# Seven products instead of eight for the first token block of a feed-forward down projection, with the up weights' sums made earlier

## The chip, the core and the metric

The kernel runs on one core of a Trainium2 chip. The metric is the device time of one execution in microseconds; lower is better. The engines that appear below are TensorE (PE; its weight loads are listed as PEld), VectorE (DVE), ScalarE (ACT), GpSimd (POOL) and SyncE (SP), which issues every DMA of this kernel.

## The reference

One layer of a hybrid encoder trunk runs over 2048 prompt positions and 32 sample positions (2080 columns here), with a width of 1024 and a hidden width of 4096, in float32:

```
h = RMSNorm(x) * (1 + scale1) + shift1        # shift, scale, gate from silu(c) @ ada_w + ada_b
p = h @ w_in                                  # mixer A: u, v; mixer B: q, k, v, z, a, b
A = u * (W_s v + b_s)                         # blocks of 128 positions
B = gated delta rule over chunks, gated RMSNorm
x = x + gate1 * (concat(A, B) @ w_out)
h = RMSNorm(x) * (1 + scale2) + shift2
x = x + gate2 * (relu(h @ w_up)^2 @ w_down)   # 1024 -> 4096 -> 1024
y = RMSNorm(x)
```

The change concerns the last product pair, `w_up` and `w_down`.

## The kernel before

**Precision.** A float32 operand of a large product is split into a high part, rounded to fp32r by a ScalarE copy, and a low part, which VectorE makes by a subtraction (`split`, `operand`). `mm3` multiplies high by high, high by low and low by high: three matmuls for one product.

**Stages.** `startup` makes the conditioning of the first normalization and the first projections. `mixers` goes through two halves of the sequence: at the head of `v_stage(0)` come the rest of the conditioning (`ada(1)`, `ada(2)`, `scale_col`), then the projections slab by slab (weights of 512 KB are loaded into `raws` and split into `wh` and `wl`), the delta rule (`delta_local`, `delta_inv` on POOL, `delta_chain`), and at the end the output projection `out_stage` of both halves. Mixer tiles are places in 25 slots of SBUF that rings hand out.

**Feed-forward.** `feed_forward` takes four token blocks b = 0 to 3 of 520 columns, each as two groups of 260. Matrices are cut into 2x2 quadrants, and a product of 2x2 by 2x2 quadrants takes seven block products instead of eight, by Winograd's form of Strassen's scheme: some sums of quadrants are multiplied instead of the quadrants, and the results are added. An up step `up(b, s)`, 16 of them, always takes seven products. For that it needs three quadrants of `w_u[s]` as they are and four sums of quadrants. In block 0 `up_weights` loads the four quadrants, POOL makes the sums, ScalarE and VectorE split them, and the high and low parts are stored to the DRAM tensors `su_d`; blocks 1 to 3 load these parts and ScalarE copies them into `uw`.

A down stage q of a block (8 of them, two half-stages u each) takes the hidden values of two up steps. `plain(b, q)` says which way it goes. All stages of block 0, and stage 7 of every block, go by `ffn_down8`: eight products, with the hidden quadrants as operands. The others go by `ffn_down`: seven products, for which `hidden` also makes the differences T1 to T4 of hidden tiles on POOL, and `down_sums` loads sums of quadrants of `w_d` from `sd_d`. These sums are made by POOL and stored: for even u in block 0 (inside `down_weights`), for odd u in block 1 (inside `down_sums`). Results are added in `add` from PSUM to `acc` by VectorE (in stage 0 the first ones are ScalarE copies). Banks of PSUM are taken and given back (`take`, `give`), eight in all. Normalized inputs of the next block are made at up step 8 (`h2_values`) and loaded and split after step 15 (`h2_load`).

**Order.** Every operation is first recorded with an engine, an estimated duration, and what it reads and writes (`Program.op`). Then `schedule` plays the engines by these estimates and puts each engine's instructions in the order of that play; this order is fixed, and each engine, SP included, follows it. Among operations that are ready the lower rank goes first:

```
CHAIN, INV, LOCAL, EVAC, GEMM, IDLE = range(6)
key = [(o.prio, due[i] if o.prio >= EVAC else i, i) ...]
```

`due` is the position of the first matmul of rank GEMM that depends on the operation. A DMA is estimated at its bytes divided by 360 bytes per ns, at least 500 ns, with 3.5 us until it lands. In the profile, instructions of these helpers have the helper's line: ScalarE L337, VectorE and POOL `tt` L352, `ts` L366, DMA L390, matmuls L398, transposes L409. Tiles tell stages apart: `g` is the PSUM of projections, `f` that of the feed-forward, C and L and B and M those of the mixers' small products; `s` is a slot, `wh`, `wl` and `wr` are places in the slab buffers and the slab staging tile.

Of the kernel before, what the change touches and what calls it, by code (L numbers as in the profile page):

```python
# [16 lines left out]
P = 128  # L17
# [37 lines left out]
CHAIN, INV, LOCAL, EVAC, GEMM, IDLE = range(6)  # L55

# [62 lines left out]
class View:  # L119
# [55 lines left out]
    def pbc(self, n):  # L175
        return self.step("partition_broadcast", np.broadcast_to(np.uint8(0), (n,) + self.shape), self.reg, n)

# [145 lines left out]
class Kern:  # L323
# [61 lines left out]
    def dma(self, out, in_, n=None):  # L385
# [4 lines left out]
        self.p.op(DMA, max(500, x), lambda: nc.sync.dma_start(out=R(out), in_=R(in_)), [out], [in_], lat=DMA_LATENCY + min(0, x - 500))  # L390
# [144 lines left out]
    def setup(self):  # L535
# [74 lines left out]
        rg("va", [(q, 256 * e) for q in (18, 19, 20) for e in range(4)][:10], (P, 256))  # L610
        rg("raw", hv(18), (P, 516))
# [24 lines left out]
        self.su_d = [[[dt(f"su_d{s}_{i}{e}", [P, 512]) for e in range(2)] for i in range(4)] for s in range(16)]  # L636
# [52 lines left out]
    def consts(self):  # L689
# [3 lines left out]
        with self.p.at(GEMM):  # L693
# [19 lines left out]
            self.fill(self.z0, 0.0)  # L713

# [208 lines left out]
    def v_stage(self, hf):  # L923
# [506 lines left out]
    def up_weights(self, b, s):  # L1430

        quad = lambda q: self.i["w_u"][s, q]
        if b == 0:
            a11, a12, a21, a22 = (self.raw(self.uraw, quad(q)) for q in range(4))
            s1, s2 = (self.turn(self.uraw) for _ in range(2))
            self.tt(s1, a21, a22, ALU.add, POOL)
            self.tt(s2, s1, a11, ALU.subtract, POOL)
        out = []

        def sum_(i, x):  # L1440
            if b == 0:
                hl = self.operand(self.uw, x)
                for e in range(2):
                    self.dma(self.su_d[s][i][e], hl[e].f32())
            else:
                hl = self.turn(self.uw)
                for e in range(2):
                    self.act(hl[e], self.raw(self.uraw, self.su_d[s][i][e]), AF.Copy)
            out.append(hl)

        plain = lambda q, x: out.append(self.operand(self.uw, x if b == 0 else self.raw(self.uraw, quad(q))))
        if b:
            s1 = s2 = s3 = s4 = a11 = a12 = a22 = None
        plain(0, a11)
        sum_(1, s2)
        sum_(0, s1)
        if b == 0:
            s3 = self.turn(self.uraw) if len(self.uraw) > 6 else a11
            self.tt(s3, a11, a21, ALU.subtract, POOL)
        sum_(2, s3)  # L1460
        if b == 0:
            s4 = s2
            self.tt(s4, a12, s2, ALU.subtract, POOL)
        sum_(3, s4)
        plain(1, a12)
        plain(3, a22)
        return out

    def down_weights(self, b, u):

        quad = lambda q: self.i["w_d"][u, q]
        if self.plain(b, u // 2):
            a = [self.raw(self.draw, quad(q)) for q in range(4)]
            out = [self.operand(self.dw, x) for x in a]
            if b == 0 and u % 2 == 0 and u < 14:
                a11, a12, a21, a22 = a
                for i, (o, x, y, op) in enumerate(((a22, a21, a22, ALU.add), (a21, a11, a21, ALU.subtract),
                                                   (a11, a22, a11, ALU.subtract), (a12, a12, a11, ALU.subtract))):
                    self.tt(o, x, y, op, POOL)
# [366 lines left out]
```

## Time and profile before

| | us |
|---|---|
| median of 3 runs | 2394.3 (2388.73 to 2394.79) |
| the profiled execution, time | 2384.64 |
| its span | 2382.9 |
| TensorE busy | 2342.0 (98%) |
| VectorE, ScalarE, POOL busy | 1722.2, 1543.3, 752.3 |
| DMA | 570.37 MB, mean 239 GB/s |

Busy time of TensorE is the time in which at least one matmul was under way. Rows of a group read: line, engine, operation, output and input tiles, shape and count, then busy us and the mean ns of one instruction, then the engine's idle time just before them and what ended it. Rows of a stretch give from:to, its length, busy us and instruction count of TensorE, its weight loads, VectorE, ScalarE and POOL, then the granted clock, the share of time that the 16 DMA engines were busy, and GB/s. Rows of a tile give a count, min/median/max ns and the first and last start in us. Rows of waits give the total us, how many times, and the longest. Rows of DMA issues give the count, the size and the median us from issue to landing.

### The profile page before, as it was taken

The page shows a single profiled execution, that of the slowest core. Times are in us where ns is not written, and L with a number is a line of the kernel's source. Part 1 is how long each engine was busy: PE and PEld are TensorE (multiplying, and loading weights), DVE is VectorE, ACT ScalarE, POOL GpSimd, SP SyncE. Part 2 cuts the span into 40 slices and gives each one's busy share as a digit, 9 for nine tenths or more (in the row PEclk, how much of TensorE's full clock was granted, in tenths as well). Part 3 has the DMA queues.
Part 4 walks back from the last instruction along what each step waited for, and adds up shares of the span by engine and source line. Part 5 has one row for each costly group of instructions (what it writes and reads, how often), then busy time and mean ns, then how long its engine had stood idle before and what let it go on. Part 6 is the DMA issues. An engine that isn't in the chain of part 4 may idle for free.

```text
span 2382.9 us, 53525 instructions
## 1 busy us (share of the span) xinstructions
PE 2342.0 (98%) x18834; PEld 2203.8 (92%) x18834; DVE 1722.2 (72%) x3993; ACT 1543.3 (65%) x3703; POOL 752.3 (32%) x1055
## 2 busy tenths in 40 slices
PE   7999999999999999999999999999999999999998
PEld 4877878999999878999999999999999999999998
DVE  5556666556664656487767778989888888778796
ACT  4555557455565434366554688787898778887774
POOL 2134421312423223354434363323531211611111
PEclk9999999999999999999999999999999999999999
DMA  8688658555457867888766778787889778886773
GB/s 310 213 288 296 215 183 261 146 185 173 152 161 231 248 200 230 270 273 273 267 228 216 255 249 302 245 299 240 289 268 297 262 251 273 251 261 225 241 238 109
DMA packets 387237, 570.37 MB, mean 239 GB/s; under 512 B 71356, under 2 KB 201296, under 8 KB 386968
## 3 DMA queue, kind: packets, MB, share of 16 engines
q1 hardware_dynamic: 386968, 566.96, 73.2%
q8 instruction: 148, 2.42, 0.4%
q14 instruction: 121, 0.99, 0.1%
HBM read 432.44 MB, written 134.35 MB: 238 GB/s over the span
## 4 chain that ended last, share of the span: by engine, by line
PE 79%; DVE 6%; DMA 6%; ACT 4%; issue 3%; POOL 2%; SPq 0%; POOLq 0%; DVEq 0%; ACTq 0%
PE f L398 43%; PE g L398 27%; PE C L398 3%; DVE s L352 3%; ACT s L337 2%; PE B L398 2%; POOL s L352 2%; PE L L398 1%; PE M L398 1%; DVE wl L352 1%; DVE s L357 1%; PE L L409 1%; ACT wh L337 1%; DMA s<-su_d 1%; DVE BL L352 1%
## 5 line engine op out<-in xcount | busy, mean ns | idle before, releaser
L337 ACT ACTIVATE s<-s 128x260 f32<-128x260 f32 (+8 forms) x1379 | 601.5, 463 | 327.9 <-DVE s L357 90.7
L398 PE MATMUL f<-s,s 128*128 128x260 f32 x4068 | 535.5, 283 | 0.4 <-DVE s L352 0.4
L398 PE MATMUL f<-BH,wh 128*128 128x260 f32 x1796 | 510.7, 284 | 5.4 <-DVE s L352 4.3
L352 POOL TENSOR_TENSOR s<-s,s 128x260 f32<-128x260 f32 (+3 forms) x354 | 356.8, 1019 | 488.1 <-ACT s L337 364.6
L398 PEld LDWEIGHTS f<-s,s 128*128 128x128 f32 x4068 | 507.2, 188 | 0.8 <-DVE s L352 0.6
L398 PE MATMUL f<-BH,wl 128*128 128x260 f32 x1796 | 507.7, 283 | 0.2 <-DVE wl L352 0.2
L398 PE MATMUL f<-BL,wh 128*128 128x260 f32 x1796 | 506.4, 282 | 0.1
L352 DVE TENSOR_TENSOR s<-s,s 128x512 fp32r<-128x512 f32 (+5 forms) x721 | 402.6, 572 | 64.6 <-ACT s L337 42.1
L352 DVE TENSOR_TENSOR s<-f,s 128x260 f32<-128x260 f32 x856 | 348.1, 420 | 118.9 <-PE f L398 109.9
L398 PE MATMUL g<-BH,wh 128*128 128x512 f32 (+2 forms) x1112 | 421.7, 379 | 0.6 <-ACT BH L337 0.4
L398 PE MATMUL g<-BH,wl 128*128 128x512 f32 (+2 forms) x1112 | 392.1, 353 | 0.0
L398 PE MATMUL g<-BL,wh 128*128 128x512 f32 (+2 forms) x1112 | 390.9, 352 | 0.9 <-DVE BL L352 0.9
L398 PEld LDWEIGHTS f<-BH,wh 128*128 128x128 f32 x1796 | 337.8, 188 | 7.9 <-DVE s L352 2.7
L398 PEld LDWEIGHTS f<-BH,wl 128*128 128x128 f32 x1796 | 338.3, 188 | 0.9 <-DVE wl L352 0.8
L398 PEld LDWEIGHTS f<-BL,wh 128*128 128x128 f32 x1796 | 338.5, 188 | 0.3 <-DVE BL L352 0.3
L352 POOL TENSOR_TENSOR s<-s 128x260 f32<-128x260 f32 (+11 forms) x315 | 157.8, 501 | 474.5 <-DVE s L352 201.1
L337 ACT ACTIVATE wh<-s 128x512 fp32r<-128x512 f32 (+1 forms) x369 | 229.7, 629 | 54.0 <-PE f L398 16.3
L398 PEld LDWEIGHTS g<-BH,wh 128*128 128x128 f32 x1112 | 210.6, 189 | 29.3 <-issue 9.3
L398 PEld LDWEIGHTS g<-BH,wl 128*128 128x128 f32 x1112 | 209.7, 189 | 19.4 <-issue 0.2
L398 PEld LDWEIGHTS g<-BL,wh 128*128 128x128 f32 x1112 | 210.9, 190 | 16.0 <-DVE BL L352 1.7
L398 PE MATMUL f<-BH,s 128*128 128x260 f32 x1016 | 224.6, 283 | 0.0
L357 DVE SCALAR_TENSOR_TENSOR s<-s,s,s 128x400 f32<-128x400 f32 (+6 forms) x318 | 164.2, 532 | 57.2 <-ACT s L337 36.4
(119 smaller groups left out, 3517.4 us busy)
## 6 DMA issues: line engine op xcount, KB each, us to landing
s<-su_d SPq DMA_DIRECT2D x288, 256.0 KB, 3.7
s<-w_u SPq DMA_DIRECT2D x171, 256.0 KB, 3.8
s<-w_d SPq DMA_DIRECT2D x151, 256.0 KB, 4.5
s<-sd_d SPq DMA_DIRECT2D x106, 256.0 KB, 4.1
wr<-su_d SPq DMA_DIRECT2D x96, 256.0 KB, 3.9
wr<-w_b SPq DMA_DIRECT2D x42, 512.0 KB, 4.3
wr<-w_d SPq DMA_DIRECT2D x70, 256.0 KB, 4.6
s<-x_d SPq DMA_DIRECT2D x128, 130.0 KB, 3.8
```

Of the source, the lines that this page charges most:

```text
L337: self.p.op(ACT, c, lambda: nc.scalar.activation(out=R(out), in_=R(in_), func=func, **{k: R(v) for k, v in kw.items()}), [out, accum], [in ...
L352: self.p.op(eng, c, lambda: e.tensor_tensor(out=R(out), in0=R(a), in1=R(b), op=op), [out], [a, b])
L357: self.p.op(DVE, c, lambda: nc.vector.scalar_tensor_tensor(out=R(out), in0=R(a), scalar=R(s), in1=R(b), op0=op0, op1=op1), [out], [a, s, b])
L398: nc.tensor.matmul(R(out), R(l), R(r), **kw)
L409: self.p.op(PE, 114, lambda: nc.tensor.transpose(R(out), R(in_), R(ident)), [out], [in_, ident])
```

## The change

1. A new `up_sums` makes the four sums of each `w_u[s]` within the mixers. It is recorded after the conditioning and its loads depend on it (`after`). Its loads have rank LOCAL, its other operations rank IDLE. Column slices of 128 are loaded, VectorE makes the sums in place and they are stored as float32 to `su_d[s][0]`; ScalarE rounds a copy, VectorE subtracts it, and the low parts go to `su_d[s][1]`. Two load places (slot 4) and four places for the low parts, in free corners of slots 8, 9, 10 and 14, are used in turn.
2. `up_weights` is the same in all blocks: three quadrants are loaded and split; for four sums two tiles are loaded and copied by ScalarE.
3. `plain` holds only for stage 7, so stages 0 to 6 of block 0 go by `ffn_down` with seven products. `down_sums` makes and stores all sums of `w_d` in block 0, for even and odd u, and block 1 loads them.
4. The differences in `hidden` run on VectorE in block 0 and on POOL in the others.
5. The staging tiles `uraw` and `draw` are one ring of eight from the start; block 0 uses the operand rings `rpa` and `rpb` of the other blocks.
6. A DMA is estimated at 330 bytes per ns in place of 360.

```diff
-        x = b / 360
+        x = b / 330
...
+        rg("sh", [(8, 512), (9, 0), (10, 768), (14, 784)], (P, 2, 128))
+        rg("sx", [(4, 0), (4, 512)], (P, 4, 128))
...
+    def up_sums(self, after):
+        for n in range(64):
+            s, c = n // 4, slice(128 * (n % 4), 128 * (n % 4) + 128)
+            x = self.new("sx")
+            with self.p.at(LOCAL):
+                self.dma(x, self.i["w_u"][s, :, :, c].rearrange("q p c -> p q c"), after=after)
+            a11, a12, a21, a22 = (x[:, q] for q in range(4))
+            self.tt(a22, a21, a22, ALU.add)
+            self.tt(a21, a11, a21, ALU.subtract)
+            self.tt(a11, a22, a11, ALU.subtract)
+            self.tt(a12, a12, a11, ALU.subtract)
+            self.dma(self.su_d[s][0][:, :, c], x)
+            for h in (slice(2, 4), slice(0, 2)):
+                y = self.new("sh")
+                self.cp(y.f32r(), x[:, h], ACT)
+                self.tt(y, x[:, h], y, ALU.subtract)
+                self.dma(self.su_d[s][1][:, h, c], y)
...
             self.scale_col(self.a2, 4, 1)
+            with self.p.at(IDLE):
+                self.up_sums((len(self.p.ops) - 1,))
...
+        for i, q in ((None, 0), (0, None), (3, None), (2, None), (1, None), (None, 1), (None, 3)):
+            if i is None:
+                out.append(self.operand(self.uw, self.raw(self.uraw, self.i["w_u"][s, q])))
+                continue
+            hl = self.turn(self.uw)
+            for e in range(2):
+                self.act(hl[e], self.raw(self.uraw, self.su_d[s][e][:, i]), AF.Copy)
...
-        if b == 1 and u % 2:
+        if b == 0:
             a11, a12, a21, a22 = (get(quad(q)) for q in range(4))
...
-    def plain(self, b, q):
-        return b == 0 or q == 7
+    def plain(self, q):
+        return q == 7
...
-        self.uraw = two(0) + two(1) + two(2)
-        self.draw = [self.raw1[0][:, 512 * e : 512 * e + 512] for e in range(2)] + two(21)
+        self.uraw = self.draw = [self.raw1[0][:, 512 * e : 512 * e + 512] for e in range(2)] + two(21) + two(0) + two(1)
...
+        eng = POOL if b else DVE
         if s % 2 == 0 and g == 0:
             put("B11", t)
-            self.tt(k0, k1, t, ALU.subtract, POOL)
+            self.tt(k0, k1, t, ALU.subtract, eng)
```

More of the change, by code (lines that the diff above doesn't have):

```diff
@@ L383, in transpose32, with dma @@
         self.p.op(DVE, 68 + 1.042 * out.n, lambda: nc.vector.transpose(R(out), R(in_)), [out], [in_])
-    def dma(self, out, in_, n=None):
+    def dma(self, out, in_, n=None, after=()):
         nc = self.nc
@@ L1428, in operand, with up_weights @@
         return hi, lo
[L1430 to L1437, printed above, removed]
-        out = []
[L1440 to L1448, printed above, removed]
-            out.append(hl)
[L1451 to L1466, printed above, removed]
+    def up_weights(self, s):
+        out = []
+        for i, q in ((None, 0), (0, None), (3, None), (2, None), (1, None), (None, 1), (None, 3)):
[5 more added lines that the diff above has]
+                self.act(hl[e], self.raw(self.uraw, self.su_d[s][e][:, i]), AF.Copy)
+            out.append(hl)
         return out
@@ L1471, in down_weights @@
         quad = lambda q: self.i["w_d"][u, q]
[L1472 to L1479, printed above, removed]
-                    self.dma(self.sd_d[u][(0, 2, 1, 3)[i]], o)
-            return out
+        if self.plain(u // 2):
+            return [self.operand(self.dw, self.raw(self.draw, quad(q))) for q in range(4)]
         return self.down_sums(b, u)
```

40 lines of the change are left out of this document (20 added, 20 removed).

## Prediction

> **What bounds the kernel now.** I read the page first: busy time by engine, then the chain that ended last.
>
> ```profile
> PE 2342.0 (98%) x18834; PEld 2203.8 (92%) x18834; DVE 1722.2 (72%) x3993; ACT 1543.3 (65%) x3703; POOL 752.3 (32%) x1055
> PE 79%; DVE 6%; DMA 6%; ACT 4%; issue 3%; POOL 2%; SPq 0%; POOLq 0%; DVEq 0%; ACTq 0%
> PE f L398 43%; PE g L398 27%; PE C L398 3%; DVE s L352 3%; ACT s L337 2%; PE B L398 2%; POOL s L352 2%; PE L L398 1%; PE M L398 1%; DVE wl L352 1%; DVE s L357 1%; PE L L409 1%; ACT wh L337 1%; DMA s<-su_d 1%; DVE BL L352 1%
> ```
>
> TensorE is nearly always busy and carries 79% of the chain; over half of that is the feed-forward products (tile f). So a matmul taken away counts in full as long as the others keep up. Where token blocks begin is seen in the first use of an up weight after a gap (rows of tile f and of tile wh in short windows):
>
> ```profile
> L398 PE MATMUL f<-BH,wh x27: 278/283/389, 1029.4 to 1039.8; 128*128 128x260 f32 x27
> L398 PE MATMUL f<-BH,wh x3: 282/282/285, 1379.2 to 1379.9; 128*128 128x260 f32 x3
> L398 PE MATMUL f<-BH,wh x2: 277/280/282, 1709.4 to 1709.8; 128*128 128x260 f32 x2
> L398 PE MATMUL f<-BH,wh x3: 282/283/285, 2040.2 to 2040.9; 128*128 128x260 f32 x3
> ```
>
> The blocks last 349.8 us (b=0), 330.2 (b=1) and 330.8 (b=2). The next rows are busy time by stage: the mixers after the conditioning, blocks 0, 1 and 2, then shorter stretches.
>
> ```profile
> core 0: us, PE busy (x) PEld busy (x) DVE busy (x) ACT busy (x) POOL busy (x), PEclk, DMA share, GB/s
> 220.00:985.00 765.00, 757.44 (x6234) 680.31 (x6233) 467.01 (x1357) 417.68 (x1157) 231.19 (x514) 1.00 0.65 203
> 1030.00:1376.00 346.00, 342.90 (x2846) 341.20 (x2845) 265.64 (x488) 202.91 (x463) 147.94 (x117) 1.00 0.76 253
> 1376.00:1707.00 331.00, 329.70 (x2739) 328.16 (x2738) 287.50 (x602) 269.60 (x617) 128.34 (x131) 1.00 0.83 272
> 1707.00:2038.00 331.00, 329.31 (x2734) 327.84 (x2733) 278.86 (x604) 269.09 (x628) 90.59 (x106) 1.00 0.83 268
> 1200.00:1300.00 100.00, 100.00 (x837) 100.00 (x836) 70.77 (x140) 51.11 (x114) 36.17 (x27) 1.00 0.66 229
> 2100.00:2300.00 200.00, 199.99 (x1664) 199.78 (x1664) 163.35 (x369) 151.10 (x339) 31.20 (x40) 1.00 0.74 240
> 1030.00:1045.00 15.00, 13.97 (x110) 13.12 (x109) 12.65 (x23) 9.96 (x26) 7.01 (x6) 1.00 0.92 299
> 1045.00:1060.00 15.00, 13.49 (x109) 12.91 (x108) 14.85 (x23) 11.56 (x27) 10.37 (x8) 1.00 0.74 235
> 1060.00:1075.00 15.00, 15.00 (x127) 14.96 (x126) 14.90 (x21) 11.11 (x26) 7.43 (x5) 1.00 1.00 352
> ```
>
> At full rate 837 matmuls take 100 us, 119.5 ns each. By the code, an up step has 7 x 4 x 3 = 84 matmuls, a down stage of seven products 2 x 28 x 3 = 168, of eight 192. Block 0 has 16 x 84 + 8 x 192 = 2880, or 344.2 us at that rate: 5.6 us are lost. Blocks 1 and 2 have 16 x 84 + 7 x 168 + 192 = 2712, 324.1 us, and lose 6.1 and 6.7. All three stand at TensorE's rate, with the clock at 1.00.
>
> **The change part by part. Seven products in block 0.** Seven stages each lose 24 matmuls: 168 x 119.5 ns = **-20.1 us**. Block 0 becomes what block 1 is, whose loss is 0.5 us higher (6.1 against 5.6): **+0.5**.
>
> **What covers this: VectorE in block 0.** The up weights' low parts fall from 7 to 3 a step; the down weights' rise from 4 to 7 a half-stage; 6 more hidden operands and 12 more PSUM additions come per stage. Block 1 already has all this, so I start from its 287.5 us. Two differences remain. The rows are groups by line and shape: three of VectorE in block 1, two of VectorE and one of POOL in block 0, one of POOL in block 1, one of VectorE at 2100 to 2300.
>
> ```profile
> L357 DVE SCALAR_TENSOR_TENSOR s<-s,nrm,s 128x260 f32<-128x260 f32 x8 | 6.7, 870 | 0.7 <-ACT s L337 0.6
> L352 DVE TENSOR_TENSOR s<-s,s 128x260 f32<-128x260 f32 x16 | 7.4, 465 | 0.1
> L352 DVE TENSOR_TENSOR s<-s,s 128x512 fp32r<-128x512 f32 x80 | 62.9, 795 | 4.6 <-ACT s L337 4.4
> L352 DVE TENSOR_TENSOR s<-s,s 128x260 f32<-128x260 f32 x8 | 5.5, 685 | 2.8 <-DMA s<-x_d 2.3 <-ACT s L337 0.4
> L352 DVE TENSOR_TENSOR wl<-s,wh 128x512 fp32r<-128x512 f32 x112 | 96.5, 872 | 16.1 <-ACT wh L337 14.5 <-DMA su_d<-wl 0.2
> L352 POOL TENSOR_TENSOR s<-s,s 128x512 f32<-128x512 f32 x47 | 67.8, 1443 | 28.9 <-DVE wl L352 25.5 <-DVE s L352 1.2
> L352 POOL TENSOR_TENSOR s<-s,s 128x260 f32<-128x260 f32 x72 | 60.6, 860 | 99.2 <-ACT s L337 83.4 <-DVE s L352 13.4 <-PE f L398 1.2
> L352 DVE TENSOR_TENSOR s<-s,s 128x512 fp32r<-128x512 f32 x54 | 36.7, 690 | 1.5 <-ACT s L337 1.5
> ```
>
> Block 0 has no final of an earlier block (-6.7), and its differences T1 to T4, 8 a stage, go to VectorE: 56 x 465 to 685 ns = 26 to 38 us. That makes 307 to 319 us in about 330: 93 to 96%, the fullest VectorE in the kernel. What is queued behind a late VectorE is in the code: a PSUM bank is given back only after its addition, so the next product waits for it. From below this costs nothing: from block 2 to block 1 VectorE rises by 8.6 us and the block stays within 0.6. From above, if all 43.5 us in which VectorE stood idle in block 1 must remain, the block needs 319 + 43.5 = 362 us, 32 more than block 1. I take **+3**, near the lower end, because the rows of whole blocks lie nearest. ScalarE comes to block 1's 270 of 331 at most.
>
> POOL in block 0 loses 64 up sums and gains 28 down sums of 1.44 us each: 148 - 92 + 40 = 96 us. Block 1 with 128 us of POOL and block 2 with 91 last the same, so POOL is covered by the products either way, and taking the odd half-stages' sums out of block 1 brings **0**. DMA: in units of 256 KB, block 0 moves 64 + 128 up transfers and 92 down now, 176 and 120 then, 12 more of 284; block 1's share of 0.83 beside a full TensorE covers it: 0.
>
> **The first steps of the feed-forward.** At 1030 to 1060 VectorE is 92% busy and TensorE issues 219 matmuls where 254 go at the rate of the next stretch: 4.1 us. The chain there runs through low parts of up weights and their stores (su_d). Those go; four of seven weights need only ScalarE copies from rows already made. But h2_load's 28 splits stay. Between 0 and -4: **-2**.
>
> **The sums in the mixers.** 64 rounds, each of one 256 KB load, four VectorE sums of 128 columns, a 256 KB store, and twice a ScalarE copy of 256 columns, a VectorE subtraction of 256 and a 128 KB store. Nearest rows of that stretch (VectorE, ScalarE), then landings, then whom TensorE waited for, first and last of seven rows (6.9 us together), the load that VectorE waited for most there, the time of an issue, and DMA in an early part:
>
> ```profile
> L352 DVE TENSOR_TENSOR s<-C,s 128x128 f32<-128x128 f32 x64 | 18.1, 283 | 0.0
> L352 DVE TENSOR_TENSOR s<-s,s 128x256 f32<-128x256 f32 x6 | 2.4, 416 | 0.0
> L337 ACT ACTIVATE s<-s 128x256 f32<-128x256 f32 x37 | 15.3, 419 | 13.1 <-DVE s L357 7.9 <-issue 4.0 <-DMA s<-xT 0.7
> s<-w_u SPq DMA_DIRECT2D x171, 256.0 KB, 3.8
> su_d<-wh SPq DMA_DIRECT2D x64, 256.0 KB, 3.5
> h_d<-s SPq DMA_DIRECT2D x16, 200.0 KB, 6.1
> PE C L409 <- DVE s L366: 3.7, 3, 2.8
> PE C L398 <- DVE s L357: 0.2, 1, 0.2
> DVE s L357 <- DMA s<-gc_d: 2.9, 3, 2.1
> L390 SPq DMA_DIRECT2D su_d<-wh x64: 319/400/760, 1028.6 to 1335.3; - x64
> 300.00:400.00 100.00, 99.05 (x953) 81.21 (x952) 63.50 (x188) 60.34 (x163) 22.29 (x47) 1.00 0.70 223
> ```
>
> VectorE: 64 x (4 x 283 + 2 x 416) ns = 126 us, 467 + 126 = 593 of 765 (78%). ScalarE: 128 x 419 ns = 54, 472 (62%). DMA: 64 x 768 KB = 50.3 MB, 143 us at the 352 GB/s that the engines moved at share 1.00; 0.65 x 765 + 143 = 640, share 0.84. SP: 256 more issues of 0.4 us, 102 us. VectorE and ScalarE stay below what block 1 bears beside a full TensorE (87% and 81%), DMA comes level with it (0.83). What stands behind: on VectorE a sum whose load is late holds the delta chain's steps; on SP a store that waits for its sum holds the loads of the chain (kq, pk) and of the next slab. From below 0; a gain is excluded, since nothing leaves this stage. From above: a load can land 2.3 us later than the usual 3.8 (6.1 is the slowest row), 64 x 2.3 = 147 us on VectorE, of whose time 172 us stay idle. I take **+4**, since TensorE waits no more than 6.9 us there now and is busy for 757 of 765: it has projection matmuls to fill with. That is far nearer the lower end.
>
> The page "SBUF — State Buffer" of the Trainium skill (section "Who interferes with whom") speaks against this place: a VectorE instruction with two SBUF inputs and a POOL instruction that reads SBUF exclude each other, and the later one waits for the whole other instruction. By that rule a sum made beside POOL's work is paid twice, on one engine or the other. The trace agrees in kind: the 512-wide subtraction took 872 ns in block 0 (POOL 43% busy) and 690 ns at 2100 to 2300 (16%). By the rule the 384 new instructions would take some 187 x 0.30/0.43 = 130 ns longer each, 50 us of VectorE, 84% in all; if a tenth of it came to TensorE, the sum would be 5 us worse than mine, 2385, still inside the forecast's own range.
>
> **The other DMA rate** (330 for 360 bytes per ns) changes only the planner's order, everywhere by a little. Its cost shows in no row; blocks 1 and 2, whose orders differ, agree to 0.6 us: 0, within 4 either way.
>
> **Sum:** -20.1 + 0.5 + 3 - 2 + 4 = -14.6 us. The profiled execution took 2384.64 (span 2382.9) and would take 2370; the runs' median lies 9.7 us above it, so the forecast is 2394.3 - 14.6 = **2380 us**.
>
> **The rivals.** *All covers hold* (VectorE and the mixers cost nothing, the start gains 4): -23.6, **2371**. For it: blocks 1 and 2; against: 93% on VectorE.
>
> *VectorE sets block 0's length*: 307 + 43.5 = 350.5, as long as before, with +4 and -2: **2397**, no change. For it: 1045 to 1060, where VectorE at 99% goes with lost matmuls; against: 1060 to 1075, at 99% too and none lost.
>
> *Slower: the sums' loads come late and hold VectorE in the mixers.* In-order VectorE stands for 147 us; if a quarter comes through, 37 us, against -18.6 for the rest: **2413**. It decides from 26 us on, somewhat over a sixth of the 147. For it: a share of 0.84 on the whole, with an early part that stands at 0.70 before anything is added; against: the load that VectorE waited for most there (gc_d) cost it 2.9 us, in three times.
>
> *The sums aren't made in the mixers:* they are last in rank on VectorE, and a round of 3.8 + 2 + 3.5 us with two tiles takes 298 us at best. If a third were left for block 0, 42 us on a VectorE at 93% would come through by more than half: +25 - 14.6, **2405**.
>
> **How the numbers follow.** Forecast 0.59, all covers 0.13, VectorE-bound 0.12, late loads 0.11, left sums 0.05. A difference of 0.3% (7.2 us) is about what can be told from none. Of the forecast's own cases 0.06 gain less than that. Faster 0.59 - 0.06 + 0.13 = 0.66; same 0.18; slower 0.16. The forecast's own range is 2372 to 2388; with the two nearest rivals 2368 to 2400 leaves out 0.16.
>
> **What would show it.** Right: 2712 matmuls of tile f in block 0 and its length 330 to 335 us; VectorE about 93% there; su_d stores between 220 and 985; VectorE near 590 us and share 0.84 in that stretch, TensorE's gaps there a few us; block 1 unchanged. Wrong: the start of block 0 later than about 1034 us (mixers), block 0 above 340 (VectorE), su_d stores after 1030 (left sums).

## The result, and the profile after

The changed kernel took **2407.5 us** (median of 5 runs, 2403.52 to 2418.17) against 2391.2 for the kernel before (5 runs beside them): a ratio of 1.0077, 95% interval 1.0057 to 1.0096. It is slower by 0.8%; 2380 had been forecast. The profiled execution took 2405.43 us, 20.8 more than that of before: of the two, that of before lies 6.6 us below its kernel's median and this one 2.1.

Busy time by engine and the chain that ended last, from the page of the changed kernel:

```profile
PE 2339.4 (97%) x18666; PEld 2189.2 (91%) x18666; DVE 1833.4 (76%) x4537; ACT 1647.9 (69%) x3981; POOL 673.4 (28%) x991
PE 57%; DMA 15%; DVE 12%; ACT 9%; issue 4%; POOL 2%; SPq 1%; DVEq 0%; ACTq 0%; POOLq 0%
```

The 168 matmuls are gone (18834 to 18666), yet TensorE is busy for only 2.6 us less, and its share of the chain that ended last falls from 79% to 57%: more of that chain now runs through DMA, VectorE and ScalarE. Where the first two token blocks begin (rows of tile wh, as for before):

```profile
L402 PE MATMUL f<-BH,wh x5: 279/287/386, 1047.6 to 1049.8; 128*128 128x260 f32 x5
L402 PE MATMUL f<-BH,wh x4: 277/282/283, 1389.9 to 1391.0; 128*128 128x260 f32 x4
```

That gives the balance by stage, each against before: block 0 begins 18.2 us later; block 0 lasts 342.3 us, 7.5 less; blocks 1 to 3 and the tail last 2403.6 - 1389.9 = 1013.7 us, 10.0 more than 2382.9 - 1379.2. Sum +20.7. Three readings follow, one for each place.

*The mixers*, busy time from 220 us to the start of block 0, then two parts of that stretch, then the worst 10 us near its end (before, then after, in each pair):

```profile
220.00:1029.40 809.40, 800.68 (x6511) 722.76 (x6509) 490.27 (x1404) 435.88 (x1198) 249.56 (x532) 1.00 0.66 206
220.00:1047.60 827.60, 806.62 (x6507) 718.22 (x6505) 581.06 (x1772) 475.06 (x1313) 251.25 (x519) 0.99 0.86 260
220.00:620.00 400.00, 397.96 (x3266) 356.10 (x3265) 251.62 (x755) 233.71 (x671) 115.60 (x279) 1.00 0.62 196
220.00:620.00 400.00, 390.85 (x3211) 343.68 (x3210) 294.30 (x935) 251.25 (x710) 114.70 (x264) 1.00 0.85 260
900.00:985.00 85.00, 81.51 (x474) 75.42 (x473) 52.67 (x117) 41.23 (x89) 31.27 (x31) 0.98 0.78 245
900.00:985.00 85.00, 77.75 (x424) 67.80 (x423) 58.54 (x151) 41.74 (x101) 22.56 (x22) 0.92 0.91 275
940.00:950.00 10.00, 6.61 (x38) 5.22 (x37) 7.37 (x16) 3.45 (x8) 5.01 (x5) 0.99 0.65 216
960.00:970.00 10.00, 3.87 (x12) 2.47 (x12) 5.12 (x14) 3.21 (x8) 2.01 (x3) 0.50 0.93 284
```

TensorE's idle time grows from 8.7 to 21.0 us, and its busy time by 5.9 us with the same instructions. Most of the new idle time comes early: it grows from 2.0 to 9.2 us between 220 and 620, from 2.0 to 4.6 between 620 and 900, and from 4.7 to 7.3 from 900 on. No engine is full: VectorE is at 70%, ScalarE at 57%, the DMA engines at 0.86. What TensorE waited for in the whole stretch (the two largest rows), and the chain near its end:

```profile
PE g L402 <- ACT BH L341: 4.1, 2, 3.5
PE C L413 <- DVE s L370: 3.0, 2, 2.6
```

```profile
948.99 2.00 SPq L394
...
953.11 4.46 DMA s<-xT
957.64 4.67 DMA s<-su_d
...
962.83 4.06 DMA s<-mix_d
966.92 0.55 ACT BH L341
967.51 66.04 PE g L402 x393
```

At the end of the mixers the output projection needs the last delta steps, written to mix_d and read back. From 949 to 967 SyncE, the DMA engines and at last ScalarE's copy carry the chain. TensorE has other matmuls until about 960 and then stands. The kernel before has such a place too: in the 10 us from 940 it is idle for 3.4 us, against 6.1 us here. From the end of this wait to block 0 it is 80 us in both (949.8 to 1029.4 before, 967.5 to 1047.6 after), so the delay of block 0 has built up before it. The clock falls in the wait: 0.50 in the ten microseconds of its gaps of 2.6 and 3.5 us. The page "TensorE: Matmul & The Clock Gate" of the Trainium skill (section "What's actually happening") has half the clock after an idle window of about 3.4 us, until a busy one; this row agrees with it.

*Block 0*: its up and down matmuls (tile f), then its first 34 us before and after, then 205 us in its middle, with the same part of block 1 of the kernel before ahead of it:

```profile
1047.50:1389.80 342.30, 333.83 (x2700) 329.58 (x2701) 111.27 (x274) 17.75 (x48) 0.99 0.85 272
1029.40:1063.70 34.30, 31.76 (x251) 30.32 (x251) 31.80 (x49) 25.68 (x64) 19.66 (x14) 1.00 0.84 273
1047.50:1081.70 34.20, 30.93 (x226) 29.98 (x227) 25.66 (x54) 31.06 (x79) 9.96 (x8) 0.90 0.88 280
1447.80:1652.80 205.00, 203.99 (x1699) 203.42 (x1698) 182.01 (x395) 162.47 (x358) 68.40 (x67) 1.00 0.82 272
1116.00:1321.00 205.00, 200.76 (x1636) 198.36 (x1635) 190.83 (x417) 156.06 (x349) 60.93 (x46) 0.99 0.84 272
```

In the first 34 us TensorE issues 25 matmuls fewer than before, 3.0 us at 119.5 ns each. VectorE has become freer there (32 to 26 us) and ScalarE nearly full: 31.06 of 34.20 us. More is lost later: in the middle TensorE issues 63 matmuls fewer (7.5 us) than in block 1 of the kernel before, which the forecast took as its model. There it is VectorE that is fuller, 190.8 us against 182.0 (93% against 89%), and ScalarE is not. TensorE's waits for ScalarE's high parts in the whole block (before, after) are half of its 8.2 us of idle time:

```profile
PE f L398 <- ACT BH L337: 0.7, 1, 0.7
...
PE f L402 <- ACT BH L341: 4.2, 3, 1.9
```

*Blocks 1 to 3*, landing times of the stored sums read into slots and of the delta chain's pk_d in before (first two rows) and after (last two):

```profile
s<-su_d SPq DMA_DIRECT2D x288, 256.0 KB, 3.7
s<-pk_d SPq DMA_DIRECT2D x32, 384.0 KB, 3.5
...
s<-su_d SPq DMA_DIRECT2D x384, 256.0 KB, 4.4
s<-pk_d SPq DMA_DIRECT2D x32, 384.0 KB, 5.7
```

The same 256 KB of a stored sum lands 0.7 us later than before, in blocks whose work on these sums has not changed; the chain's own loads in the mixers land 2.2 us later.

### The profile page after: what moved, and what is told of

It reads as the page before. It is cut to its first block, busy times and chain, and to the rows that moved or that the text cites. A ratio compares the mean times of both kernels' runs of the same rounds, so it can differ in the third digit from the quotient of the medians.

```text
span 2403.6 us, 54281 instructions
## 1 busy us (share of the span) xinstructions
PE 2339.4 (97%) x18666; PEld 2189.2 (91%) x18666; DVE 1833.4 (76%) x4537; ACT 1647.9 (69%) x3981; POOL 673.4 (28%) x991
## 4 chain that ended last, share of the span: by engine, by line
PE 57%; DMA 15%; DVE 12%; ACT 9%; issue 4%; POOL 2%; SPq 1%; DVEq 0%; ACTq 0%; POOLq 0%
PE f L402 29%; PE g L402 20%; DVE s L356 7%; ACT s L341 5%; DMA s<-su_d 3%; PE C L402 3%; DMA wr<-su_d 2%; DVE s L361 2%; DMA s<-w_u 2%; POOL s L356 1%; ACT wl L341 1%; ACT wh L341 1%; PE B L402 1%; DVE wl L356 1%; SPq L394 1%
## 5 line engine op out<-in xcount | busy, mean ns | idle before, releaser
L341 ACT ACTIVATE s<-s 128x260 f32<-128x260 f32 (+11 forms) x1576 | 678.1, 461 | 321.0 <-DVE s L356 104.0
L356 DVE TENSOR_TENSOR s<-s,s 128x260 fp32r<-128x260 f32 (+6 forms) x960 | 501.2, 537 | 93.9 <-ACT s L341 75.7
L402 PEld LDWEIGHTS f<-s,s 128*128 128x128 f32 x3900 | 494.9, 189 | 5.7 <-DVE s L356 3.3
L356 DVE TENSOR_TENSOR s<-f,s 128x260 f32<-128x260 f32 x928 | 372.6, 418 | 96.2 <-PE f L402 89.8
L356 POOL TENSOR_TENSOR s<-s,s 128x260 f32<-128x260 f32 (+3 forms) x309 | 291.9, 956 | 477.3 <-ACT s L341 370.3
L356 POOL TENSOR_TENSOR s<-s 128x260 f32<-128x260 f32 (+11 forms) x304 | 147.8, 486 | 459.3 <-ACT s L341 220.3
L341 ACT ACTIVATE wh<-s 128x512 fp32r<-128x512 f32 (+1 forms) x352 | 218.0, 628 | 46.8 <-DMA s<-su_d 29.2
L402 PE MATMUL f<-BH,s 128*128 128x260 f32 x1016 | 236.3, 285 | 4.2 <-ACT BH L341 4.2
L402 PEld LDWEIGHTS g<-BH,wl 128*128 128x128 f32 x1112 | 210.2, 189 | 20.7 <-issue 1.3
L361 DVE SCALAR_TENSOR_TENSOR s<-s,s,s 128x512 f32<-128x512 f32 (+5 forms) x318 | 162.2, 528 | 38.8 <-ACT s L341 22.5
```

Of the source, the lines that this page charges most:

```text
L341: self.p.op(ACT, c, lambda: nc.scalar.activation(out=R(out), in_=R(in_), func=func, **{k: R(v) for k, v in kw.items()}), [out, accum], [in ...
L356: self.p.op(eng, c, lambda: e.tensor_tensor(out=R(out), in0=R(a), in1=R(b), op=op), [out], [a, b])
L361: self.p.op(DVE, c, lambda: nc.vector.scalar_tensor_tensor(out=R(out), in0=R(a), scalar=R(s), in1=R(b), op0=op0, op1=op1), [out], [a, s, b])
L402: nc.tensor.matmul(R(out), R(l), R(r), **kw)
```

## Experiments

Ratios are against runs of the kernel before on the same chip (medians 2390.9 to 2392.8 us). "Block 0 begins" is the first row of tile f with wh after the gap, as above.

### 1. Which part costs it: the sums taken away, and split in two

No sums at all (`e1`); up steps load plain weights in the sums' place, at the same sizes:

```diff
-            with self.p.at(IDLE):
-                self.up_sums((len(self.p.ops) - 1,))
...
-                self.act(hl[e], self.raw(self.uraw, self.su_d[s][e][:, i]), AF.Copy)
+                self.act(hl[e], self.raw(self.uraw, self.i["w_u"][s, (i + e) % 4]), AF.Copy)
```

> The changed kernel with up_sums left out altogether; the feed-forward loads quadrants of w_up in place of the stored sums, so its up steps have the same transfers and copies but other numbers. Changed kernel: block 0 begins at 1047.6 us, before 1029.4; block 0 lasts 342.3 us, before 349.8. Theory 'the mixers pay': block 0 begins at 1026 to 1031 and the total is 2380 to 2390 us, with block 0 still near 340 because VectorE is full there. Theory 'the order pays' (the DMA rate and all that is placed anew): block 0 begins at 1040 or later although no sum is made. Theory 'block 0 pays for leftovers of the mixers': block 0 falls to 332 or less.

Measured: 2379.56 us, 0.9944 (0.9925 to 0.9963).

Transfers alone (`e2`): no sums are worked out, and the loaded weights are stored in their place:

```diff
-            self.tt(a22, a21, a22, ALU.add)
...
-                self.cp(y.f32r(), x[:, h], ACT)
-                self.tt(y, x[:, h], y, ALU.subtract)
-                self.dma(self.su_d[s][1][:, h, c], y)
+                self.dma(self.su_d[s][1][:, h, c], x[:, h])
```

> The changed kernel with the transfers of up_sums all in place, but without its VectorE sums, ScalarE copies and VectorE subtractions: the tiles are stored as loaded. Theory 'transfers' (51 MB more in the mixers, landing of the chain's loads late, SP's queue longer): block 0 begins at 1043 to 1050 as in the changed kernel. Theory 'VectorE' (131 us more in its fixed order, 22 us of it waiting for loads): block 0 begins at 1028 to 1034. Half by each: about 1038.

Measured: 2404.03 us, 1.0045 (1.0029 to 1.0061).

Calculation alone (`e3`): every instruction and every DMA issue kept, but loads (after the first two) and stores of one partition; up steps load plain weights as in `e1`:

```diff
+                    self.dma(x[0:1], self.i["w_u"][s, :, 0:1, c].rearrange("q p c -> p q c"), after=after)
...
-            self.dma(self.su_d[s][0][:, :, c], x)
+            self.dma(self.su_d[s][0][0:1, :, c], x[0:1])
...
```

> The changed kernel with all VectorE and ScalarE work of up_sums, and as many DMAs, but each after the first two loads moves one partition only (2 KB and less), so almost no bytes; the feed-forward loads quadrants of w_up in place of the sums. Theory 'transfers': block 0 begins at 1027 to 1033. Theory 'VectorE': at 1042 to 1050. Theory 'SP' (192 issues more, each 0.4 to 0.5 us, in one queue): also 1040 or later, and then the run with transfers alone is late as well.

Measured: 2374.82 us, 0.9928 (0.9906 to 0.9951). Start of block 0 in e1 and e3, the mixers' busy time in both, and block 0's in e1:

```profile
L402 PE MATMUL f<-BH,wh x8: 281/283/388, 1031.5 to 1034.8; 128*128 128x260 f32 x8
L402 PE MATMUL f<-BH,wh x7: 282/284/387, 1032.8 to 1035.7; 128*128 128x260 f32 x7
220.00:1031.50 811.50, 800.51 (x6504) 719.10 (x6502) 482.05 (x1385) 430.48 (x1179) 233.57 (x519) 0.99 0.66 202
220.00:1032.80 812.80, 800.11 (x6513) 720.71 (x6511) 583.34 (x1775) 473.10 (x1315) 252.57 (x522) 0.99 0.67 205
1031.40:1374.40 343.00, 333.20 (x2707) 328.95 (x2708) 315.29 (x658) 267.15 (x619) 107.55 (x86) 0.99 0.85 272
```

What follows: 101 us more of VectorE and 43 us more of ScalarE in the mixers move block 0's start by 1.3 us, and the run is no slower for them. The sums' *work* is free where next to no bytes go with it; so are 256 more issues on SyncE. The cost comes in with the transfers, and without them seven products gain 13 to 18 us. Block 0 lasts 343 us even with no sums, so its shortfall is its own.

### 2. The sums added to the kernel before

`e7`: `up_sums` put at the same place in the kernel before, storing to tensors that nothing reads:

```diff
+            with self.p.at(IDLE):
+                self.up_sums((len(self.p.ops) - 1,))
```

> The kernel before, at its own DMA rate, with up_sums added in the mixers and stored to tensors that nobody reads; the feed-forward is that of before, with eight products in block 0. Theory 'transfers in the mixers': block 0 begins 10 to 18 us later than 1029.4, total 2402 to 2412. Theory 'pitch of the stored sums' carries most of the loss: block 0 begins within 6 us and blocks 0 to 3 last as before, total 2393 to 2399.

Measured: 2405.46 us, 1.0072 (1.0055 to 1.009); block 0 begins at 1048.1. The sums' price does not hang on the rest of the change: 15 us here, with nothing read back.

### 3. How the sums lie in memory

A sum i was stored as a slice of `[P, 4, 512]`: each row of 2 KB lies 8 KB from the next. `e5` keeps each sum in one piece:

```diff
+            t = self.dr.tile([4 * P, 512], F32, name=name)
+            return Mem(2048).view(0, (P, 4, 512), lambda: t.rearrange("(i p) c -> p i c", i=4))
```

> The changed kernel with one edit: the DRAM tensor of the stored sums holds four whole 128x512 matrices one behind the other, so that the feed-forward reads each as 256 KB in one piece, as before, and not in rows of 2 KB at a pitch of 8 KB. Stores keep their number, bytes and 512-byte runs. In the changed kernel the loads s<-su_d land after 4.4 us (median; before 3.7), blocks 1 to 3 take 1013.8 us, and 1002.4 without the sums. Theory 'pitch' (the layout slows the reads and with them blocks 1 to 3): landing 3.7 to 3.9, blocks 1 to 3 at 1002 to 1006, total 2393 to 2399. Theory 'mixers alone' (the later blocks differ by the order they got): landing and blocks as in the changed kernel, total 2403 to 2410.

Measured: 2396.11 us, 1.0017 (1.0004 to 1.0029). `e15` makes the same edit to e2.

> Transfers of the sums alone (no sums are worked out, so what is stored are the loaded weights), in rows of 512 B, each stored sum in one piece. Against the whole rows (2386.0 us) only the row length differs; against transfers alone with the pitch of 8 KB (2404.0 us) only the pitch. If the pitch is worth 11 us here as it was with the work: 2393 us. If rows of 512 B cost nothing by themselves: 2386 us.

Measured: 2385.72 us, 0.9971 (0.996 to 0.9982). First use in block 1 and the span of e2, e15 and e5, then the landing of stored sums in e15 and e5:

```profile
core 0 of [0], span 2403.3 us
L402 PE MATMUL f<-BH,wh x4: 278/282/283, 1387.5 to 1388.6; 128*128 128x260 f32 x4
core 0 of [0], span 2383.8 us
L402 PE MATMUL f<-BH,wh x4: 277/282/283, 1380.7 to 1381.8; 128*128 128x260 f32 x4
core 0 of [0], span 2396.0 us
L402 PE MATMUL f<-BH,wh x3: 277/282/283, 1393.0 to 1393.7; 128*128 128x260 f32 x3
s<-su_d SPq DMA_DIRECT2D x384, 256.0 KB, 4.0
s<-su_d SPq DMA_DIRECT2D x384, 256.0 KB, 3.9
```

From block 1 to the end: 1015.8 us pitched against 1003.1 in one piece (transfers alone), 1013.7 against 1003.0 (the whole change). Before it was 1003.7. The pitch is the whole loss of blocks 1 to 3, 11 us with the work and 18 us in the medians without it (where block 0 gains too). The stores have the pitch too, but they are over before block 0. In the mixers one piece gains nothing: block 0 begins at 1051.3 in e5 and at 1039.3 in e15 (1037.9 in e2).

### 4. Row length

`e9`: transfers alone, in one piece, in rows of 2 KB and 1 KB in place of 512 B. `e14`: the same rows with all the work (sums of other elements). `e16`: only the loads in 2-KB rows, from a second layout of the weights.

```diff
-                self.dma(x, self.i["w_u"][s, :, :, c].rearrange("q p c -> p q c"), after=after)
+                self.dma(x.re("p q c -> p (q c)"), self.i["w_k"][s, n % 4], after=after)
```

> Transfers alone again (no sums, no copies, no subtractions in the mixers), with as many bytes and issues, but each load and store is a whole 128x512 matrix or half of one: rows of 2 KB and 1 KB in place of 512 bytes. The stored tensors are flat. Transfers with short rows took 2404.0 us, no sums 2379.6; the flat tensor alone took 11 us off the changed kernel. Theory 'short rows' (98304 rows of 512 bytes hold the 16 DMA engines): block 0 begins at 1027 to 1033, total 2378 to 2384. Theory 'bytes' (50 MB, whatever their rows): block 0 begins 6 us or more after 1031.5, total 2388 to 2396.

Measured: 2385.98 us, 0.9978 (0.9965 to 0.9991).

> The changed kernel with each stored sum in one piece, all work of the sums done, but the sums' loads and stores made in rows of 2 KB and 1 KB instead of 512 B (so the sums are of other elements: a part of the computation is changed). Same bytes, same number of issues, same waits. If the short rows carry the cost: block 0 begins near 1039 us as with whole transfers alone, about 2386 us. If it is the bytes together with the work: 1048 to 1052 us and 2392 to 2397 us.

Measured: 2393.69 us, 1.0007 (0.9996 to 1.0018).

> The changed kernel with each stored sum in one piece, and the 64 loads of the sums taken from a second layout of the up weights in which one round's four blocks lie side by side, in rows of 2 KB; the stores keep rows of 512 B. A whole kernel. If short rows carry the cost, half of the short packets are gone and with them about half of what whole rows would give: 2390 us. If loads are what makes sums late (the sum waits for the load, nothing waits for the store until block 0): nearly all of it, 2386 to 2388 us. If rows do not matter beside the work: 2393 to 2397 us.

Measured: 2393.86 us, 1.0005 (0.9994 to 1.0017).

Whole rows (e9) and 512-byte rows (e15) take the same time without the work, and nearly the same with it (e14, e16, e5). Row length is not the cause; my guess of half the gain for e16 fell. What stands is that work and transfers together cost 8 to 10 us more than transfers alone, though the work alone costs nothing:

```profile
220.00:1039.30 819.30, 801.38 (x6505) 718.84 (x6503) 478.19 (x1387) 431.12 (x1183) 242.13 (x519) 0.99 0.87 262
220.00:1047.70 827.70, 807.90 (x6512) 722.31 (x6510) 584.40 (x1776) 475.20 (x1313) 254.56 (x521) 0.99 0.84 261
```

These are the mixers of e15 and e14: 2 us of the difference are idle time of TensorE, 6.5 us busy time with the same instructions.

### 5. Queue, order, place, amount

`e13`: the sums' stores issued by ScalarE's queue.

```diff
+            self.p.op(ACT, 60, lambda: nc.scalar.dma_start(out=R(out), in_=R(in_)), [out], [in_], lat=DMA_LATENCY)
```

> The changed kernel with each stored sum in one piece, and the 192 stores of the sums issued from ScalarE's queue instead of SyncE's. It tells whether SyncE's order (a store that waits for its sum holds the loads behind it) turns the transfers into lost time. Theory A (the queue of SyncE: transfers alone and calculation alone cost little, both together 18 us at the start of block 0, because each slow load makes a sum late and each late sum holds SyncE): block 0 begins near 1038 us, as with transfers alone, and the time is about 2384 us. Theory B (the DMA engines are simply fuller, SyncE's waits are not what counts): block 0 begins at 1048 to 1052 as before, 2393 to 2398 us. ScalarE issuing could also hold ScalarE itself: later than 1055 us and above 2400.

Measured: 2430.73 us, 1.0159 (1.0141 to 1.0178); block 0 begins at 1075.8. Whom TensorE waited for in the mixers:

```profile
PE L L416 <- ACT s L341: 4.7, 5, 1.7
PE L L405 <- ACT s L341: 4.5, 7, 2.2
PE C L405 <- ACT s L341: 4.3, 5, 1.8
```

Theory A got no support: ScalarE's copies for the delta chain now keep TensorE waiting (13.5 us in these three rows, 3.6 in e5's), as ScalarE too works in order. The run has a price of its own and so says little of SyncE; e3 says more, where SyncE has as many issues and waits for the same sums at no cost.

`e17`: the planner is told that the sums' loads take 3 us longer. `e8`: these loads at the lowest rank.

```diff
-lat=DMA_LATENCY + min(0, x - 500), after=after)
+lat=DMA_LATENCY + min(0, x - 500) + (3000 if after else 0), after=after)
... (e8)
-            with self.p.at(LOCAL):
+            with self.p.at(IDLE):
```

> The changed kernel with each stored sum in one piece; the planner is told that the loads of the sums land 3 us later than it thought, so that VectorE's fixed order puts each sum behind the time at which its load has really landed. Nothing else changes. If VectorE's waits for the sums' loads (22.4 us in 17 waits) are what makes work and transfers together dear: the waits go, block 0 begins near 1040 us and the time is about 2386 us. If fuller DMA engines and a fuller VectorE delay the delta chain whatever the order: 2392 to 2398 us. Other orders of the same work have differed by 1 to 3 us.

Measured: 2424.83 us, 1.0124 (1.0105 to 1.0142).

> The changed kernel with the loads of up_sums at rank IDLE instead of LOCAL, so that the planner places them only where the DMA queue has nothing else; bytes unchanged. Theory 'bytes' (the mixers have no room for 51 MB): block 0 begins at 1043 or later, or the sums run on into block 0; total 2403 to 2412. Theory 'rank' (the loads push the chain's and slabs' loads aside): block 0 begins at 1036 or earlier, total 2390 to 2400.

Measured: 2446.14 us, 1.0247 (1.0228 to 1.0265). VectorE's wait for the sums' loads in the changed kernel and in e17; then, of e17, the start of block 0, the stores of sums, and what TensorE waited for in the 76 us after that start:

```profile
DVE s L356 <- DMA s<-w_u: 22.4, 17, 3.2
...
DVE s L356 <- DMA s<-w_u: 2.6, 2, 1.4
L402 PE MATMUL f<-BH,wh x10: 280/283/388, 1044.0 to 1047.8; 128*128 128x260 f32 x10
L394 SPq DMA_DIRECT2D su_d<-s x192: 359/452/2836, 285.2 to 1107.6; - x192
PE f L402 <- ACT s L341: 14.1, 2, 13.6
```

The waits went, and block 0 began 7 us earlier than in e5, where a theory of late loads wanted 11. But the sums got later and later: the last is stored at 1107.6 us, within block 0, and the first up steps stand (14.1 us behind ScalarE's copies of stored sums). In e8 the last store is at 1108.2 us, and the price is higher. So the changed order is already near the point where sums are left over (its last store is at 1042.7, 5 us before block 0).

`e10`: 32 of the 64 rounds, in the first half; `e18`: the same 32 rounds begun in the second half of the mixers. Steps 8 to 15 load plain weights.

```diff
-        for n in range(64):
+        for n in range(32):
```

> The changed kernel with the flat tensor and only the first 32 of 64 rounds of up_sums: 25 MB. Up steps 8 to 15 load quadrants of w_up in place of stored sums, with the same transfers and copies. Flat with all sums 2396.1, none 2379.6. Theory 'bytes, each alike': half of the loss, 2386 to 2390, block 0 beginning near 1040. Theory 'a full queue' (harmless until the DMA engines have no room): 2378 to 2384, block 0 at 1034 or earlier.

Measured: 2394.25 us, 1.0006 (0.9994 to 1.0019); block 0 begins at 1050.5.

> The changed kernel with each stored sum in one piece and 32 of the 64 rounds of sums, as in the run with half of the sums, but begun in the second half of the mixers instead of the first; the up steps 8 to 15 load the plain up weights in place of the sums that are not made (a part of the computation is left out). Half of the sums in the first half gave 2394.3 us, as much as all of them. If the place counts (the first half's delta chain is where they hurt): 2382 to 2386 us. If any sums push the mixers past a point from which the end is ordered worse: 2392 to 2396 us again.

Measured: 2390.68 us, 0.9997 (0.9987 to 1.0007); block 0 begins at 1041.2. Half of the sums cost as much as all of them in one piece (2396.1). In the profiled executions the later place begins block 0 by 9 us earlier; in the medians 3.6 us are left and the intervals overlap, so a gain from the place is not shown. The end of the mixers in e10:

```profile
900.00:985.00 85.00, 73.50 (x392) 64.57 (x391) 49.95 (x123) 37.09 (x89) 20.95 (x23) 0.88 0.73 225
```

In e10 the last sum is stored at 598.5 us. At the end the DMA share (0.73) is then below that of the kernel before (0.78), and yet TensorE is idle for 11.5 us there, against 7.3 in the change and 5.2 in e1. So neither the amount of the sums nor transfers at the end explain the delay of block 0 by themselves. Nor does one place: before 620 us TensorE is idle for 9.2 us in the change, 9.8 in e5 and 9.7 in e10, but for 4.2 in e14 and 4.3 in e18, which lose 12.2 and 11.6 us between 900 and 985.

### 6. The other parts of the change

`e4`: the kernel before with the other rate.

```diff
-        x = b / 360
+        x = b / 330
```

> The kernel before with the planner's DMA rate at 330 instead of 360, nothing else. Theory 'the order pays': 2395 to 2405 us. Theory 'the mixers pay': within 0.2% of before, 2386 to 2396, block 0 beginning at 1025 to 1033.

Measured: 2391.68 us, 0.9993 (0.998 to 1.0007). Nothing, as forecast.

`e6`: the differences T1 to T4 of block 0 on POOL.

```diff
-        eng = POOL if b else DVE
+        eng = POOL
```

> The changed kernel with the differences T1 to T4 of block 0 on POOL as in the other blocks. VectorE in block 0 falls from 88% by some 25 us to about 81%. Theory 'VectorE sets block 0': block 0 falls from 342.3 us to 333 or less and the total by 8 or more. Theory 'the start of block 0 and late loads' (9 us lost in its first tenth, the rest in single gaps behind ScalarE's high parts): block 0 stays at 339 to 346, total within 4 us of 2407.

Measured: 2413.27 us, 1.0105 (1.0076 to 1.0133), 6 us above the change, with intervals that just overlap; block 0 lasts 347.9 us. The run does not relieve VectorE, though: its busy time in block 0 stays at 303.3 us (302.5 in the change) with 58 instructions fewer, as its subtractions of two operands in SBUF became slower (the change, then e6):

```profile
L356 DVE TENSOR_TENSOR s<-s,s 128x512 fp32r<-128x512 f32 x76 | 56.0, 745 | 4.7 <-ACT s L341 4.6
L356 DVE TENSOR_TENSOR s<-s,s 128x512 fp32r<-128x512 f32 x76 | 61.8, 823 | 8.0 <-ACT s L341 7.4
```

POOL is busy for 151.2 us in block 0 of e6 and for 104.6 in the change. VectorE's additions from PSUM (tile f) took 417 and 418 ns and did not change. So the place on VectorE is the better one of the two, and whether VectorE's load costs block 0 its time is not tested.

`e11`: seven products in block 0 without the move: its up sums are made on POOL and split within block 0, as before, but with the changed kernel's one ring of eight staging tiles. `e12`: the same in only four of the seven stages (0, 2, 4, 6), whose `plain` is shown.

```diff
-    def plain(self, q):
-        return q == 7
+    def plain(self, b, q):
+        return q == 7 or b == 0 and q not in (0, 2, 4, 6)
```

> The changed kernel without up_sums in the mixers: POOL makes the up weights' sums within block 0 and ScalarE and VectorE split them there, as before the change; all seven stages of block 0 keep seven products. Flat tensor. VectorE in block 0 would be 266 us (before) plus about 59 for more down weights, operands and additions, and 26 for the differences: 350, with TensorE needing 324. Theory 'VectorE sets block 0 then': block 0 lasts 350 us or more, total 2385 to 2400. Theory 'it fits': block 0 at 340 to 345, total 2376 to 2383.

Measured: 2470.19 us, 1.0328 (1.0303 to 1.0353).

> The same, but only stages 0, 2, 4 and 6 of block 0 go by seven products, the others by eight as before; sums of w_down for the others are made in block 1. TensorE saves 96 matmuls, 11.5 us; VectorE in block 0 would be 266 + 4/7 of 85 = 315 us of 340 (93%). Theory 'VectorE at 92% costs 9 to 12 us' as in the run without sums: block 0 at 342 to 348, total 2383 to 2390. Theory 'only a full VectorE costs': block 0 at 337 to 341, total 2378 to 2383.

Measured: 2412.23 us, 1.0081 (1.0057 to 1.0105). Block 0 in e11 and in e12:

```profile
1032.80:1469.80 437.00, 374.84 (x2708) 353.37 (x2707) 398.21 (x716) 246.65 (x553) 201.09 (x148) 0.94 0.67 220
1032.30:1407.00 374.70, 350.39 (x2779) 342.09 (x2780) 341.47 (x621) 224.14 (x515) 163.17 (x123) 0.98 0.72 239
```

VectorE is 91% busy in both, and block 0 lasts 437 and 375 us. As written here, seven products do not pay without the move. That VectorE is the reason, since it has to split the up sums in the block in which it also adds and splits for seven products, is argued: the shared staging ring is another difference from the kernel before, and no run takes it away.

No version of the change here beats the kernel before and computes all of it: the nearest, e16 and e5, take 2393.9 and 2396.1 us. The 2375 to 2386 us of e1, e3, e9 and e15 are of kernels that leave part of the sums out.

## Why the prediction was wrong, step by step

- **168 matmuls, -20.1: right.** The count fell by 168, and without the sums the gain shows: 2379.6 us.
- **The step that failed: "The sums in the mixers ... I take +4".** They cost 28 us in all (2407.5 against e1's 2379.6). The quantities were sized well: 126 us of VectorE forecast and 101 measured (e3 against e1), a DMA share of 0.84 forecast and 0.86 measured. Their effect was not. *About 11 us are the pitch* of the stored sums, paid in blocks 1 to 3, which the forecast had as unchanged: "four of seven weights need only ScalarE copies from rows already made" priced the reading of stored sums at nothing and never asked how their rows lie (e5, e15). *About 16 us lie in the mixers.* The ground for +4 was that TensorE "has projection matmuls to fill with". The waits were not filled: against e1, TensorE's idle time in the mixers rose from 11.0 to 21.0 us and its busy time from 800.5 to 806.6, over the whole stage and not in one place. Some 6 us of this come with the bytes alone (2385.7 against 2379.6), 8 to 10 more when the work is added (2393.7 to 2396.1). Half of the sums cost as much as all of them (e10), which no term of the forecast's sum allowed for.
- **VectorE in block 0, +3, and the first steps, -2: mis-sized together by 11 us.** VectorE came out near the forecast (307 to 319 us; 302.5 in the change, 315.3 in e1). Forecast 331.2 us, measured 342.3, and 343.0 without the sums. At the start the forecast took VectorE's relief for a gain and put no price on ScalarE, which now copies eight tiles of stored sums a step beside the 28 first splits: 25.7 to 31.1 us of 34. Instead of 2 us won, 3.0 were lost there, 5 of the 11. Most of the rest lies in the middle of the block, where VectorE is at 93% and 7.5 us more are lost than in block 1 of the kernel before; the forecast's +3 stood for this. "Block 0 above 340 (VectorE)" was the named sign, and it came. The rows point to ScalarE at the start and leave VectorE possible in the middle; no run takes either load away, as e6 left VectorE as busy as it was.
- **The other rate, 0: right** (e4).
- **The rivals.** *Late loads hold VectorE* gave 2413, close to the result, but it asked for 26 us to come through out of 147; the waits were 22.4 us, and taking nearly all of them away moved block 0's start by 7 us (e17). It is at most a part, not the cause. *Sums left over* did not happen in the change (last store 1042.7) and did in e8 and e17, where it cost 29 us (e17 beyond e5) and 39 us (e8 beyond the change). *VectorE sets block 0's length* gave 350.5 us for the block and 342.3 were measured; as a part of that loss it is not excluded.
- **The rule on shared access** (the Trainium skill's page "SBUF — State Buffer", section "Who interferes with whom") asked for some 130 ns more in each new instruction. The row of the 128-column sums in the mixers:

```profile
L356 DVE TENSOR_TENSOR s<-s 128x128 f32<-128x128 f32 x256 | 75.9, 298 | 25.3 <-DMA s<-w_u 22.4
```

  298 ns against the 283 that the forecast took: 15 ns, not 130, and e3 shows all this work at no cost, so in the mixers the rule changed little. In block 0 the trace agrees with it: with POOL busier in e6, the subtractions of two operands in SBUF took 823 ns in place of 745, and the additions from PSUM stayed as they were.
- **Open.** Why work and transfers together cost more than each alone is not settled. SyncE's issues and waits (free in e3), row length (e14, e15) and VectorE's late loads (e17, at most 7 us) don't carry it by themselves; that chain steps behind slower landings meet a fuller VectorE fits the rows of the change, and is not shown. A rival stands beside it: the planner sees other operations in each kernel and gives each a fixed order of its own (in e1 to e3 too), e8 and e17 show that an order can cost 29 to 39 us, and no run keeps the order of the mixers while it takes the sums away. Nor is it known why TensorE's busy time grows by 6 us with the same instructions, beyond its lower clock.

## What to carry to other kernels

Do not price a moved step by the mean shares of the stage that takes it: with the DMA engines at 0.86 and VectorE at 70%, TensorE's idle time in that stage still went from 8.7 to 21.0 us. Split the step into its work and its transfers and run each alone; here the two together cost more than the sum of both. When a tensor is stored to be read many times, ask how its rows lie and count its readers: the pitch cost 11 of the 28 us. When one engine is relieved, look at the next fullest in the same 30 us, and when work moves from VectorE to POOL, look whether VectorE's busy time falls at all.

## What the runs showed of the hardware

Reading 256 KB into a slot in 128 rows of 2 KB at a pitch of 8 KB took 4.3 to 4.4 us to land (e2, the change), against 3.9 to 4.0 in one piece (e5, e15), and the kernel with 512 such reads took 18 us longer with transfers alone (e2 1.0045, e15 0.9971). No run uses another pitch, so the pitch itself and the mere gaps between the rows are not told apart. The page "DMA: Bandwidth & Descriptors" of the Trainium skill (section "Latency and other measured facts") tells of a loss at row pitches of large powers of two, from 2 MiB on with pieces of 16 KiB; here a loss comes at 8 KB, with pieces of 2 KB; whether it has the same cause no run shows.

Rows of 512 B were no dearer than rows of 2 KB and 1 KB (e15 2385.7 us, e9 2386.0). The same page of the Trainium skill (section "Specifications") has 512 B as the smallest transfer at line rate; the runs agree.

In block 0, VectorE's 512-wide subtraction of two operands in SBUF took 745 ns with POOL busy for 31% of the time and 823 ns at 43% (the change, e6); its addition with one input from PSUM took 418 and 417 ns.
